# Rotary embedding on split heads: the cos and sin tables in 8 descriptors of 8 KB on partitions 0 to 31

## The chip, the cores and the metric

The kernel runs on one core of a Trainium2 chip. The core has a matrix engine (TensorE, PE in the profile), a vector engine (VectorE, DVE), a scalar engine (ScalarE, ACT), GpSimd (POOL) and SyncE (SP), which here only issues transfers. 16 DMA engines move data between the chip's memory (HBM) and the core's on-chip memory of 128 partitions. The metric is the device time of one execution in microseconds.

## The reference

```python
batch, seq, dim = 16, 512, 1024          # x: float32
num_heads = 16                           # head_dim 64, half_dim 32
# cos, sin: [seq, half_dim], float32
x = x.reshape(batch, seq, num_heads, head_dim)
x1, x2 = x[..., :half_dim], x[..., half_dim:]
cos = cos[None, :, None, :]
sin = sin[None, :, None, :]
rotated = np.concatenate([
    x1 * cos - x2 * sin,
    x1 * sin + x2 * cos
], axis=-1)
```

Every element of x is read once and every element of the output written once: 33.55 MB each way. cos and sin are 64 KB each; all batches and all heads share them, so a row of the tables belongs to a position in the sequence.

## The kernel before, in words

**Tiling.** The input is cut into 8 slabs of two batches each. A slab is 4.19 MB of float32: 128 partitions of 8192 numbers (32 KB), eight consecutive positions of the sequence (`rpp` = 8) per partition. Five float32 buffers hold slabs (`slots` = 5). Two bfloat16 buffers (`xpool`, tag "xb", 16 KB per partition) hold the slab that is being worked on.

**Loads and stores.** SP issues the loads of slabs 0 to 5 (line 64), POOL those of slabs 6 and 7. Loads 0 to 4 are issued at the start, load 0 first. Load s + 5 reuses the buffer of slab s and so waits until store s has landed. ACT issues the stores (line 151), and at the start, behind load 0, the two table loads (line 80).

**Tables.** Partition p needs the table rows of its own eight positions, and partitions 64 apart need the same ones. The kernel does not load them in that form. It loads each table as `TR` = 16 rows of 1024 float32 (4 KB): cos to partitions 0, 8, ..., 120 of the tile `raw`, sin to partitions 4, 12, ..., 124. `raw` has been set to zero before by DVE (line 72), and POOL casts it to bfloat16 (`raw_b`, line 102). Then TensorE spreads the rows: POOL has built one-hot matrices in `pick` (a memset, line 92, and 12 selects, line 96; three kinds g for cos, sin and minus sin, and `TQ` = 4 quarters j of a row), and for each of four parts of the accumulator `acc` four matmuls (line 107) pick for every partition the row and quarter that it needs: 16 matmuls of 128 by 128 by 256. DVE copies `acc` to the bfloat16 table `tab` (line 113). Every multiply reads `tab`.

**Work on a slab.** ACT casts it to bfloat16 (line 122). DVE multiplies twice by parts of `tab` (line 143; the product with the sine goes into the slab's own buffer) and adds with the halves exchanged (line 146). ACT casts the result back to float32 into the slab's buffer (line 149) and issues the store. Slabs 0, 6 and 7 are worked on in two halves, the others whole. ACT's order is written out by the loop: the cast of the next piece, then the write-back of the current one, then the store.

There is no planner. Each engine and each queue does its instructions in the order of the program, and each instruction waits for the data and buffers that it needs.

Of the kernel before, what the change touches and what calls it, by code (L numbers as in the profile page):

```python
# [2 lines left out]

# [4 lines left out]


@with_exitstack  # L10
def kernel(
    ctx: ExitStack,
    tc: tile.TileContext,
    x: bass.AP,
    cos: bass.AP,
    sin: bass.AP,
    num_heads: int,
    out: bass.AP,
):
    nc = tc.nc  # L20
    P = nc.NUM_PARTITIONS

    batch, seq, dim = x.shape
    nh = num_heads
    hd = dim // nh
    half = hd // 2
    bf16 = mybir.dt.bfloat16
    f32 = mybir.dt.float32

    nb = 2  # L30
    slots = 5
    nslabs = batch // nb
    rpp = nb * seq // P
    W = rpp * dim
    SP = seq // rpp
    TW = rpp * half

    out_flat = out.rearrange("b s h d -> b s (h d)")

    singles = ctx.enter_context(tc.tile_pool(name="singles", bufs=1))  # L40
    slabs = ctx.enter_context(tc.tile_pool(name="slabs", bufs=slots))
    xpool = ctx.enter_context(tc.tile_pool(name="xpool", bufs=2))
    psum = ctx.enter_context(tc.tile_pool(
        name="psum", bufs=1, space=bass.MemoryType.PSUM))


    def dram(t, s, a=0, n=W):
        return bass.AP(tensor=t.tensor, offset=t.offset + s * nb * seq * dim + a,
                       ap=[[W, P], [1, n]])


    def view(t, offset, *dims):
        return dataclasses.replace(t, offset=t.offset + offset,
                                   ap=[t.ap[0], *[list(d) for d in dims]])


    slab = {}


    def load(s):  # L60

        queue = nc.sync if s < nslabs - 2 else nc.gpsimd
        slab[s] = slabs.tile([P, W], f32, tag="slab", name="slab")
        queue.dma_start(out=slab[s], in_=dram(x, s))  # L64

    TR = 16
    TQ = seq // TR // rpp
    TC = seq * half // TR  # L70
    raw = singles.tile([P, TC], f32, tag="raw")
    nc.vector.memset(raw, 0.0)  # L72


    def load_tables(queue):
        for i, src in enumerate((cos, sin)):
            to = dataclasses.replace(
                raw, offset=raw.offset + 4 * i * raw.ap[0][0],
                ap=[[P // TR * raw.ap[0][0], TR], [1, TC]])
            queue.dma_start(out=to, in_=bass.AP(  # L80
                tensor=src.tensor, offset=src.offset, ap=[[TC, TR], [1, TC]]))


    load(0)
    load_tables(nc.scalar)
    for s in range(1, slots):
        load(s)

    pick = singles.tile([P, 3 * TQ * P], bf16, tag="pick")
    nc.gpsimd.memset(pick, 0.0)  # L92
    for g in range(3):
        for j in range(TQ):
            part = view(pick, (g * TQ + j) * P + j, (SP, P // SP), (TQ, TR))
            nc.gpsimd.affine_select(  # L96
                out=part, in_=part, compare_op=mybir.AluOpType.not_equal,
                fill=-1.0 if g == 2 else 1.0, base=-4 if g else 0,
                pattern=[[0, P // SP], [-(P // TR), TR]], channel_multiplier=1)

    raw_b = singles.tile([P, TC], bf16, tag="raw_b")
    nc.gpsimd.tensor_copy(out=raw_b, in_=raw)  # L102

    acc = psum.tile([P, 2 * rpp * hd], f32, tag="acc")
    for g, at in ((0, 0), (0, half), (1, rpp * hd), (2, rpp * hd + half)):
        for j in range(TQ):
            nc.tensor.matmul(  # L107
                view(acc, at, (hd, rpp), (1, half)),
                view(pick, (g * TQ + j) * P, (1, P)),
                view(raw_b, j * TW, (half, rpp), (1, half)),  # L110
                start=j == 0, stop=j == TQ - 1)
    tab = singles.tile([P, 2 * rpp * hd], bf16, tag="tab")
    nc.vector.tensor_copy(out=tab, in_=acc)  # L113

    xb = {}


    def cast(u):
        s, r, n = u
        if r == 0:  # L120
            xb[s] = xpool.tile([P, W], bf16, tag="xb", name="xb")
        nc.scalar.copy(out=view(xb[s], r * dim, (1, n * dim)),  # L122
                       in_=view(slab[s], r * dim, (1, n * dim)))

    passes = []
    for s in range(nslabs):
        n = rpp if 1 <= s < nslabs - 2 else rpp // 2  # L130
        passes += [(s, r, n) for r in range(0, rpp, n)]


    cast(passes[0])
    for i, (s, r, n) in enumerate(passes):
        if i + 1 < len(passes):
            cast(passes[i + 1])
        xs = view(slab[s], r * dim, (1, n * dim))
        xu = view(xb[s], r * dim, (1, n * dim))

        t2 = view(slab[s].bitcast(bf16), 2 * r * dim, (1, n * dim))
        for t, a in ((t2, rpp * hd), (xu, 0)):
            nc.vector.tensor_mul(  # L143
                out=t, in0=xu,
                in1=view(tab, a + r * hd, (hd, n), (0, nh), (1, hd)))
        nc.vector.tensor_add(  # L146
            out=xu, in0=xu, in1=view(t2, half, (hd, n * nh), (-half, 2), (1, half)))

        nc.scalar.copy(out=xs, in_=xu)  # L149
        if r + n == rpp:  # L150
            nc.scalar.dma_start(out=dram(out_flat, s), in_=slab[s])  # L151
            if s + slots < nslabs:
                load(s + slots)


# [1 line left out]
_INS = ['x', 'cos', 'sin', 'num_heads']  # L157
_OUTS = [((16, 512, 16, 64), 'float32')]

_NUMBERS = {'num_heads': 16}  # L160


# [26 lines left out]
```

## Time and profile before

| | |
|---|---|
| median of 3 runs | 162.08 us (161.93 to 162.35) |
| span of the profiled execution, first to last instruction | 161.0 us |
| moved | 67.24 MB, mean 418 GB/s |
| busy: ACT, DVE, POOL, PE | 113.6, 109.3, 5.9, 3.6 us |
| sin table landed, after its issue | 10.3 us |
| first multiply starts | 19.02 us |
| stores issued (slab 0, 1, 2, 7) | 38.10, 52.90, 67.25, 146.00 us |

The profiled execution is listed by its span; what the median has above it, 1.1 us, lies outside the first and last instruction. The profile's time line is in microseconds from the start of the span. A row of it gives start, duration, engine, line, operation, output and inputs, and in brackets how long the engine had been idle and what ended that. A stretch of time gives the busy time of each engine in it, the clock that TensorE was granted, the busy share of the 16 DMA engines, and GB/s; a packet is counted where it starts, so a short stretch can show a share slightly over 1. The DMA rows give a queue (q1 for SP's transfers, q10 for ACT's, q0 for POOL's), its packets, MB, and the time of its packets as a share of 16 engines over the stretch. A slab's packet is a partition's 32 KB. Packets of a few bytes are the completions.

### The profile page before, as it was taken

To read this page: it belongs to the slowest core of one execution; us is meant where nothing else is said; L and a number is where in the kernel's file an instruction comes from. 1 tells how busy PE (TensorE), PEld (TensorE's weight loads), DVE (VectorE), ACT (ScalarE), POOL (GpSimd) and SP (SyncE) were. 2 spreads that over 40 slices of the span, in tenths; PEclk is the share of its full clock that TensorE was granted. 3 is DMA by queue.
4 is the path that set the end of the run, shared out by engine and by line. 5 is a ranking of instruction groups with operands and counts; after the bars stand their busy time and mean duration, and the time that the engine had idled before them with its cause. 6 is when DMAs were issued, how large, how long until landed. Compare 5 with 4: busy or idle time off the path is not lost.

```text
span 161.0 us, 204 instructions
## 1 busy us (share of the span) xinstructions
PE 3.6 (2%) x16; PEld 2.3 (1%) x16; DVE 109.3 (68%) x35; ACT 113.6 (71%) x23; POOL 5.9 (4%) x20
## 2 busy tenths in 40 slices
PE   0005300000000000000000000000000000000000
PEld 0003100000000000000000000000000000000000
DVE  2000599999999969997998089949739599930000
ACT  2104939998999899899926998089995999562000
POOL 8002000000000000000010001000000000000000
DMA  6999999999999999999999999999999999999993
GB/s 228 423 383 423 399 464 440 399 456 440 407 432 456 415 423 456 423 415 464 391 415 432 456 415 432 448 423 432 448 423 432 440 432 432 440 423 440 440 423 147
DMA packets 2368, 67.24 MB, mean 418 GB/s; under 512 B 288, under 2 KB 288, under 8 KB 320
## 3 DMA queue, kind: packets, MB, share of 16 engines
q10 hardware_dynamic: 1216, 33.69, 48.5%
q1 hardware_dynamic: 864, 25.17, 37.2%
q0 software_dynamic: 288, 8.39, 12.1%
HBM read 33.69 MB, written 33.55 MB: 418 GB/s over the span
## 4 chain that ended last, share of the span: by engine, by line
DMA 42%; DVE 21%; ACT 20%; issue 4%; PE 2%; POOL 1%; ACTq 1%; POOLq 0%; DVEq 0%
DMA out_dram<-slab 20%; DMA slab<-in_x_dram 15%; ACT slab L149 13%; DVE xb L143 7%; DVE slab L143 7%; ACT xb L122 7%; DMA raw<-in_sin_dram 6%; DVE xb L146 6%; PE acc L107 2%; DVE tab L113 1%; POOL raw_b L102 1%; DVE raw L72 1%; ACTq L80 0%; ACTq L151 0%; POOLq L102 0%
## 5 line engine op out<-in xcount | busy, mean ns | idle before, releaser
L122 ACT CAST xb<-slab 128x4096 bf16<-128x4096 f32 (+1 forms) x11 | 56.6, 5155 | 25.3 <-DMA slab<-in_x_dram 24.1
L149 ACT CAST slab<-xb 128x4096 f32<-128x4096 bf16 (+1 forms) x11 | 56.6, 5154 | 3.8 <-DVE xb L146 3.8
L143 DVE TENSOR_TENSOR slab<-xb,tab 128x4096 bf16<-128x4096 bf16 (+1 forms) x11 | 35.9, 3260 | 15.5 <-ACT xb L122 15.3
L146 DVE TENSOR_TENSOR xb<-xb,slab 128x4096 bf16<-128x4096 bf16 (+1 forms) x11 | 35.9, 3260 | 0.3
L143 DVE TENSOR_TENSOR xb<-xb,tab 128x4096 bf16<-128x4096 bf16 (+1 forms) x11 | 35.9, 3260 | 0.3
L113 DVE CAST tab<-acc 128x1024 bf16<-128x1024 f32 x1 | 1.2, 1225 | 15.8 <-PE acc L107 15.8
L64 POOL DMA_DIRECT2D slab<-in_x_dram x2 | 1.2, 611 | 85.4 <-DMA out_dram<-slab 66.8
L107 PE MATMUL acc<-raw_b,pick 128*128 128x256 bf16 x16 | 3.6, 418 | 14.1 <-POOL raw_b L102 14.1
L122 ACT ACT_TABLE_LOAD x1 | 1.3, 1283 | 3.2 <-issue 3.2
L107 PEld LDWEIGHTS <-pick 128*128 128x128 bf16 x16 | 2.3, 145 | 14.9 <-issue 11.5
L96 POOL TENSOR_SCALAR_AFFINE_SELECT pick<-pick 128x32 bf16<-128x32 bf16 x12 | 2.1, 248 | 0.1
L72 DVE MEMSET raw<- 128x1024 f32 x1 | 0.9, 912 | 1.0 <-PEq L170 1.0
L92 POOL MEMSET pick<- 128x1536 bf16 x1 | 1.4, 1379 | 0.3 <-POOLq L170 0.3
L102 POOL CAST raw_b<-raw 128x1024 bf16<-128x1024 f32 x1 | 1.0, 1037 | 8.7 <-DMA raw<-in_sin_dram 8.7
L170 POOL MEMSET const-float32-0.0<- 128x1 f32 x1 | 0.1, 99 | 0.2 <-issue 0.2
L170 POOL MEMSET const-bfloat16-1.0<- 128x1 bf16 x1 | 0.1, 102 | 0.0
L170 POOL MEMSET const-uint8-127<- 128x1 uint8 x1 | 0.1, 102 | 0.0
L170 POOL MEMSET const-float32-1.0<- 128x1 f32 x1 | 0.1, 99 | 0.0
## 6 DMA issues: line engine op xcount, KB each, us to landing
out_dram<-slab ACTq DMA_DIRECT2D x8, 4096.0 KB, 26.1
slab<-in_x_dram SPq DMA_DIRECT2D x6, 4096.0 KB, 28.2
slab<-in_x_dram POOLq DMA_DIRECT2D x2, 4096.0 KB, 24.5
raw<-in_cos_dram ACTq DMA_DIRECT2D x1, 64.0 KB, 8.1
raw<-in_sin_dram ACTq DMA_DIRECT2D x1, 64.0 KB, 10.3
```

The source lines that it names most:

```text
L64: queue.dma_start(out=slab[s], in_=dram(x, s))
L72: nc.vector.memset(raw, 0.0)
L92: nc.gpsimd.memset(pick, 0.0)
L96: nc.gpsimd.affine_select(out=part, in_=part, compare_op=mybir.AluOpType.not_equal, fill=-1.0 if g == 2 else 1.0, base=-4 if g else 0, pat ...
L102: nc.gpsimd.tensor_copy(out=raw_b, in_=raw)
L107: nc.tensor.matmul(view(acc, at, (hd, rpp), (1, half)), view(pick, (g * TQ + j) * P, (1, P)), view(raw_b, j * TW, (half, rpp), (1, half)), ...
L113: nc.vector.tensor_copy(out=tab, in_=acc)
L122: nc.scalar.copy(out=view(xb[s], r * dim, (1, n * dim)), in_=view(slab[s], r * dim, (1, n * dim)))
L143: nc.vector.tensor_mul(out=t, in0=xu, in1=view(tab, a + r * hd, (hd, n), (0, nh), (1, hd)))
L146: nc.vector.tensor_add(out=xu, in0=xu, in1=view(t2, half, (hd, n * nh), (-half, 2), (1, half)))
L149: nc.scalar.copy(out=xs, in_=xu)
L170: nc = _bacc.Bacc("TRN2", target_bir_lowering=False, num_devices=1)
```

## The change

Each table is loaded as 8 rows of 2048 float32 (8 KB) instead of 16 rows of 4 KB: cos to partitions 0, 4, ..., 28 and sin to 1, 5, ..., 29. The rows, in float32 and as bfloat16, no longer have tiles of their own. They lie in one of the two "xb" buffers, which is not in use at that time and becomes the buffer of slab 1 afterwards. DVE's memset and POOL's cast now work on 32 partitions and 2048 columns, where they had 128 partitions and 1024 columns. A row now holds eight groups of positions (`TQ` = 8), so there are 24 selects of 16 elements instead of 12 of 32, `pick` is twice as long (3072 columns), and 32 matmuls, with 32 rows each, take the place of 16 with 128 rows.

```diff
-    TR = 16
+    TR = 8
+    TS = 4
+    TK = TR * TS
     TQ = seq // TR // rpp
     TC = seq * half // TR
-    raw = singles.tile([P, TC], f32, tag="raw")
-    nc.vector.memset(raw, 0.0)
+    tmp = xpool.tile([P, W], bf16, tag="xb", name="tmp")
+    raw = view(tmp.bitcast(f32), 0, (1, TC))
+    raw_b = view(tmp, 2 * TC, (1, TC))
+    nc.vector.memset(raw[0:TK], 0.0)
...
             to = dataclasses.replace(
-                raw, offset=raw.offset + 4 * i * raw.ap[0][0],
-                ap=[[P // TR * raw.ap[0][0], TR], [1, TC]])
+                raw, offset=raw.offset + i * raw.ap[0][0],
+                ap=[[TS * raw.ap[0][0], TR], [1, TC]])
...
-                fill=-1.0 if g == 2 else 1.0, base=-4 if g else 0,
-                pattern=[[0, P // SP], [-(P // TR), TR]], channel_multiplier=1)
+                fill=-1.0 if g == 2 else 1.0, base=-1 if g else 0,
+                pattern=[[0, P // SP], [-TS, TR]], channel_multiplier=1)
...
-    raw_b = singles.tile([P, TC], bf16, tag="raw_b")
-    nc.gpsimd.tensor_copy(out=raw_b, in_=raw)
+    nc.gpsimd.tensor_copy(out=raw_b[0:TK], in_=raw[0:TK])
...
             nc.tensor.matmul(
                 view(acc, at, (hd, rpp), (1, half)),
-                view(pick, (g * TQ + j) * P, (1, P)),
-                view(raw_b, j * TW, (half, rpp), (1, half)),
+                view(pick, (g * TQ + j) * P, (1, P))[0:TK],
+                view(raw_b, j * TW, (half, rpp), (1, half))[0:TK],
                 start=j == 0, stop=j == TQ - 1)
```

## The prediction

> **What bounds the kernel now.** Read the page first: its span, the three rows of busy engines, the row of DMA and the bytes. Then the stretches of time, to see whether the transfers ever pause.
>
> ```profile
> span 161.0 us, 204 instructions
> DVE  2000599999999969997998089949739599930000
> ACT  2104939998999899899926998089995999562000
> DMA  6999999999999999999999999999999999999993
> HBM read 33.69 MB, written 33.55 MB: 418 GB/s over the span
> ```
>
> ```profile
> 0.00:1.80 1.80, 0.00 (x0) 0.00 (x0) 0.78 (x1) 0.00 (x0) 1.27 (x5) 1.00 0.21 55
> 6.00:12.00 6.00, 0.00 (x0) 0.00 (x0) 0.00 (x0) 0.00 (x0) 0.00 (x0) 1.00 1.07 421
> 20.00:40.00 20.00, 0.00 (x0) 0.00 (x0) 19.90 (x8) 16.98 (x5) 0.00 (x0) 1.00 1.02 437
> 100.00:124.00 24.00, 0.00 (x0) 0.00 (x0) 17.76 (x7) 17.54 (x4) 0.53 (x1) 1.00 1.00 433
> 149.00:157.00 8.00, 0.00 (x0) 0.00 (x0) 0.00 (x0) 0.00 (x0) 0.00 (x0) 1.00 1.01 438
> ```
>
> The last two columns are the DMA share and GB/s. Once the first slab is on its way, all 16 DMA engines work without a pause at 420 to 438 GB/s until about 158 us. 67.24 MB at 433 GB/s is 155.3 us, so the span of 161.0 is that, 1.8 us before the first byte, and about 4 us of slow start, uneven finish and last landing. The transfers bound the kernel. DVE and ACT rest for tens of microseconds each. The span lies 1.1 us under the median of the runs, 162.08; I add that 1.1 to every sum.
>
> The change works in the first 24 us, in what leads to the first multiply:
>
> ```profile
> 1.02 0.91 DVE L72 MEMSET raw<- 128x1024 f32 x1 [1.02 <-PEq L170]
> 1.96 0.56 ACTq L80 DMA_DIRECT2D raw<-in_cos_dram  x1
> 2.56 0.61 ACTq L80 DMA_DIRECT2D raw<-in_sin_dram  x1
> 12.99 1.04 POOL L102 CAST raw_b<-raw 128x1024 bf16<-128x1024 f32 x1 [8.72 <-DMA raw<-in_sin_dram]
> 14.08 3.57 PE L107 MATMUL acc<-raw_b,pick 128*128 128x256 bf16 x16 [14.08 <-POOL raw_b L102]
> 17.69 1.23 DVE L113 CAST tab<-acc 128x1024 bf16<-128x1024 f32 x1 [15.76 <-PE acc L107]
> ```
>
> Each waits for the one above; the first multiply starts at 19.02 us. While they wait, the DMA engines are loading slabs 0 to 4, for which nothing here is needed.
>
> **The change, part by part, on the path to the first multiply.**
> - Memset: 1024 f32 columns took 0.91 us; 2048 on 32 partitions take 0.91 (if partitions counted) to 1.82. I take 1.82: +0.91 on the issue of both tables.
> - Landing: cos landed 8.1 us after its issue, sin 10.3, though 64 KB need 0.15 us at 433 GB/s. They wait in turn behind 32 KB slab packets of 1.2 us each. The later issue adds 0.91, or a whole turn of 1.2, or nothing if the packet still catches its turn; and only 8 of the descriptors' owners must answer instead of 16, so the slowest may drop out, a turn less. I take 0, with -1.2 and +1.2 as ends.
> - Cast on POOL: 1.04 us for 1024 columns, so 2.07 for 2048: +1.04 (0 if partitions counted).
> - Picking tables: the memset of 1536 columns took 1.38 us, 3072 take 2.76; 24 selects at the 0.17 us spacing of the present 12 take 4.2. POOL is done at 7.7 instead of 4.3 us, under its 8.7 us wait for sin: 0.
> - Matmuls: 16 take 3.57 us, one every 0.21. Their moving side stays 256 columns, so 32 take 6.93: +3.36 (0 if 32 rows were four times as fast).
> - The copy to tab has the same shape: 0.
>
> Sum: first multiply at 19.02 + 1.04 + 3.36 = 23.4 us, 4.4 later (ends -1.2 and +5.8). The Trainium skill (TensorE: Matmul & The Clock Gate, Part 1: The HAM clock gate (the "warmup" mystery)) has TensorE at half clock for some 3.4 us of steady work and at full clock after. By it the second 16 matmuls would take about 1.7 us, an estimate, and the sum would be 2.7 instead of 4.4. The page's clock column stands at 1.00 and the 16 matmuls here show no step, but their burst is only 3.57 us long, so no run here shows it.
>
> The shared buffer adds one wait: ACT's cast of slab 1 (24.04 us, when the slab lands) now waits for the last matmul. That ends near 17.67 + 4.4 = 22.1, 1.9 us earlier. Behind that cast stand ACT's two write-backs of slab 0, which wait for DVE anyway: 0; if matmuls end after 24.0, the cover is gone.
>
> **What the 4.4 us do further on.** DVE's pass over slab 0 ends at 37.0 instead of 32.6, so ACT's second write-back (3.6 us) ends at 40.6 and store 0 is issued 2.5 us later than 38.1, since ACT had to wait for nothing there before but its own cast. Stores 1, 2 and 3 come the full 4.4 later (57.3, 71.7, 86.0). None of this empties the DMA queues: five slabs are 20.97 MB, 48.4 us at 433 GB/s, so loads alone last until about 51 us, and store 0 could be 10 us late. Store 0 landed at 61.5 (issue 38.1 and 23.4), load 4 at about 64 (longest time to landing, 61.3, from its issue near 2.8). Together they carry the same bytes in either order, so store 0 lands no later than 64: load 5 is issued 0 to 2.5 us later, and I take 1.3. Loads 5, 6 and 7 follow one another at half rate (cast at 85.95, 105.32, 124.68), so slab 7 arrives about 1.3 later too, and from there it is a bare chain to the last store: 146.00 becomes 147.3.
>
> ```profile
> 124.68 3.60 ACT L122 CAST xb<-slab 128x4096 bf16<-128x4096 f32 x1 [1.82 <-DMA slab<-in_x_dram]
> 142.37 3.60 ACT L149 CAST slab<-xb 128x4096 f32<-128x4096 bf16 x1 [3.47 <-DVE xb L146]
> 146.00 0.34 ACTq L151 DMA_DIRECT2D out_dram<-slab  x1
> out_dram<-slab ACTq DMA_DIRECT2D x1, 4096.0 KB, 14.1
> ```
>
> Does that show at the end? The last store landed 14.1 us after its issue. Its own 4.19 MB need 9.7 us, the first load shows 1.0 us from issue (0.74) to first byte (about 1.75), and I put 0.5 on its final receipt: so it queued 2.9 us behind store 6. With engines that finish over about 1.2 us (the DMA share is 0.99 from 157 to 158 us and 0.31 in the next), 1.7 us of lateness cost nothing. 1.3 is inside: 0 us.
>
> **What the tables take from the DMA engines.** This is on the path. Beside them the slab packets slow down:
>
> ```profile
> q1 hardware_dynamic: 73, 2.39, 101.0%
> q10 hardware_dynamic: 62, 0.13, 5.9%
> ...
> q1 hardware_dynamic: 299, 8.75, 101.6%
> ```
>
> The first two rows are 6 to 12 us, the last 20 to 40 (32 of its 299 packets are completions). 73 packets in 101% of 96 engine-us are 1.33 us each, against 1.22 later: 0.11 x 73 / 16 = 0.5 us lost per engine. The tables' own packets take 5.9% of 6 us, 0.35 us per engine. An 8 KB descriptor is twice a 4 KB one, and eight of them leave some engines without. An engine with one of each table gives 0.7 us instead of 0.35, one without gives 0; on both, the 0.5 may stay (same bytes), vanish (fewer packets) or double (twice the size). So the engine with tables changes by -0.15 to +0.85, the one without by -0.85 to +0.15. The last engine sets the end; no view here names it. With the 0.5 unchanged it is +0.35 or -0.35, and I take 0 between.
>
> Sum: 161.0 + 0 + 0 = 161.0 in the span, 162.1 us as the runs count. The forecast is no change: within 0.3% (0.5 us), which is about what a measurement of this kernel can tell from none.
>
> **Rivals.**
> - **Tables cost the DMA engines less.** Fewer and larger packets disturb the slabs less, and the last engine is one without tables. For it: the slow packets lie exactly where the tables do. Against: the bytes are the same. The most is 0.85; I price it at 0.6: 161.5 us.
> - **Tables crowd eight engines.** If an engine's loss grows with the table bytes that it carries itself, 0.85 becomes 1.7 on eight engines, and one of these ends last: 162.9 us. Against it: the 0.5 now falls on packets ahead of an engine's own table too. The Trainium skill (DMA: Bandwidth & Descriptors, Rules for kernel authors) speaks against the change here: a copy whose outermost dimension is under 16 runs on no more engines than that. No run of before has such a copy; by it each of the eight carries 16 KB and the rest none, as assumed in this rival.
> - **The last store is late.** If the 4.4 us pass whole to slab 7, the last store is issued at 150.4, and 4.4 less the 1.7 to 2.9 of slack is 1.5 to 2.7: about 164.1 us. It decides from 147.7 us on. For it: the chain of waits does run from the tables through ACT to the last store. Against: that chain passes twice through transfers that share a full pipe, and the bound on store 0 cuts it to 2.5.
> - **The split is undone.** If the 8 rows were cut into 16 pieces again, the DMA side is as before and the 4.4 us hidden: 162.1, part of the forecast.
>
> **How the numbers follow.** Forecast 0.47 (0.42 within 0.3%, 0.03 below, 0.02 above), cheaper tables 0.24, crowding 0.14, late store 0.15. So faster 0.27, same 0.42, slower 0.31. The forecast's own range is 161.6 to 162.6. The range of 161.2 to 163.4 takes in the full 0.85 gained, crowding, and the mild end of the late store, and leaves out about 0.14 above and 0.05 below.
>
> **What the changed profile would show.** Memset 1.8 us, POOL cast 2.1, 32 matmuls 5 to 7 us, first multiply 22 to 24.5, store 0 near 40.6: right about the start. Last store at 146 to 147.7 and DMA at 430 GB/s or more throughout: right about the cover. Wrong if DMA falls below that between 40 and 150 us, if the last store lands within 11.5 us of its issue (nothing ahead of it), or if the slab packets between 6 and 13 us take far more or less than 1.33 us.

## The result, and the profile after

The changed kernel takes 163.34 us (median of 22 runs, 162.58 to 164.12); the kernel before, run in turn with it, 162.36 us (22 runs, 161.93 to 163.31). The ratio is 1.0048, with an interval of 1.0035 to 1.0062: **slower by 0.5%, 0.8 us**. The two medians are 1.0 us apart; the text goes by the ratio. The forecast was no change, within 0.3%, at 162.1 us. The measured change is larger than that and clear of the noise; the time lies just inside the stated range of 161.2 to 163.4 us.

The profiled execution has a span of 162.1 us and took 163.86 us, so 1.8 us lie around the span. From its page:

```profile
span 162.1 us, 263 instructions
DMA  7999999989999999998999999999999999999990
q14 instruction: 1, 0.01, 0.0%
HBM read 33.69 MB, written 33.55 MB: 415 GB/s over the span
DMA packets 2337, 67.25 MB, mean 415 GB/s; under 512 B 272, under 2 KB 272, under 8 KB 272
```

The DMA row has no gap: transfers still bound the kernel. One row is new: a single packet on a queue of kind "instruction", of which the page of before has none. In the trace it is 8 KB and starts at 162.06 us, as the span ends. The row of packets of before, for comparison:

```profile
DMA packets 2368, 67.24 MB, mean 418 GB/s; under 512 B 288, under 2 KB 288, under 8 KB 320
```

The time line of the changed kernel (start, duration, engine, line, operation, in brackets the wait before it):

```profile
1.22 1.76 DVE L76 MEMSET tmp<- 32x2048 f32 x1 [1.22 <-PEq L173]
3.02 1.22 ACTq L84 DMA_DIRECT2D tmp<-in_cos_dram  x1
3.47 3.87 POOL L100 TENSOR_SCALAR_AFFINE_SELECT pick<-pick 128x16 bf16<-128x16 bf16 x24
...
13.32 1.88 POOL L105 CAST tmp<-tmp 32x2048 bf16<-32x2048 f32 x1 [5.98 <-DMA tmp<-in_sin_dram]
...
15.25 6.98 PE L110 MATMUL acc<-tmp,pick 32*128 32x256 bf16 x32 [15.25 <-POOL tmp L105]
...
22.27 1.23 DVE L116 CAST tab<-acc 128x1024 bf16<-128x1024 f32 x1 [19.28 <-PE acc L110]
...
23.59 2.29 DVE L146 TENSOR_TENSOR slab<-xb,tab 128x4096 bf16<-128x4096 bf16 x1
...
40.86 0.35 ACTq L154 DMA_DIRECT2D out_dram<-slab  x1
...
62.45 0.33 SPq L64 DMA_DIRECT2D slab<-in_x_dram  x1
...
146.34 0.34 ACTq L154 DMA_DIRECT2D out_dram<-slab  x1
```

The first multiply starts at 23.59 us, 4.57 later than before; store 0 is issued at 40.86, 2.8 later; load 5 at 62.45, 0.9 later. The last store is issued only 0.34 us later than before. The last row of the issues gives how long it then took to land:

```profile
out_dram<-slab ACTq DMA_DIRECT2D x1, 4096.0 KB, 14.3
```

Before, that was 14.1 us. Stretches of time in the changed kernel (the last two columns are the DMA share and GB/s):

```profile
20.00:40.00 20.00, 2.23 (x11) 1.18 (x9) 17.57 (x8) 13.92 (x4) 0.00 (x0) 1.00 0.99 429
40.00:60.00 20.00, 0.00 (x0) 0.00 (x0) 19.81 (x6) 16.96 (x4) 0.00 (x0) 1.00 1.01 419
...
100.00:124.00 24.00, 0.00 (x0) 0.00 (x0) 20.09 (x8) 21.11 (x5) 0.53 (x1) 1.00 1.00 433
124.00:146.00 22.00, 0.00 (x0) 0.00 (x0) 18.16 (x8) 18.40 (x6) 0.00 (x0) 1.00 1.00 433
...
157.00:158.00 1.00, 0.00 (x0) 0.00 (x0) 0.00 (x0) 0.00 (x0) 0.00 (x0) 1.00 1.06 459
...
159.00:160.00 1.00, 0.00 (x0) 0.00 (x0) 0.00 (x0) 0.00 (x0) 0.00 (x0) 1.00 0.15 66
```

No stretch pauses, and 100 to 124 us moves 433 GB/s as before. From 40 to 60 us it moves less than before, at about the same share:

```profile
40.00:60.00 20.00, 0.00 (x0) 0.00 (x0) 18.97 (x5) 19.25 (x3) 0.00 (x0) 1.00 0.99 428
```

The end differs too: 66 GB/s for a microsecond is two packets of 32 KB, started while most engines are done. In the profiled execution of before that microsecond is empty, but so it is in the second profile of the changed kernel (`a0_after` below).

What becomes of the last 2 us is read from the instructions of the program's last source line, its closing (durations in ns as min/median/max, then first and last start in us). Before:

```profile
L184 POOLq DRAIN  x3: 34/93/24737, 100.0 to 160.7; - x3
L184 SPq DRAIN  x3: 7/7/7, 160.2 to 160.5; - x3
L184 POOLq EVENT_SEMAPHORE_RANGE_CLEAR  x1: 139/139/139, 160.5 to 160.5; - x1
```

And in the changed kernel:

```profile
L187 POOLq DRAIN  x3: 40/230/24290, 100.7 to 161.8; - x3
L187 SPq DRAIN  x3: 7/7/7, 160.8 to 161.1; - x3
L187 POOLq EVENT_SEMAPHORE_RANGE_CLEAR  x1: 139/139/139, 161.6 to 161.6; - x1
```

SP begins to drain when the last store has landed: at 160.2 before, at 160.8 now. POOL clears the semaphores 0.3 us later before, 0.8 us later now. So the 1.1 us between these two spans are 0.6 of a later landing and **0.5 of a longer closing**, in which no data move. In the trace the step is plain: when the last engine has been released from the barrier that follows SP's DRAIN, POOL's own DRAIN ends 0.12 us later in before and 0.62 us later now. Of these 0.5 us, 0.14 are the DRAIN itself (230 ns in place of 93); 0.36 pass before it starts, and nothing in the trace names what POOL does in them. The 0.6 of later landing is one execution against another; the 0.5 is what the experiments below test.

### The profile page after: what moved, and what is told of

Same layout as the page of the kernel before. It is cut to its first block, busy times and chain, and to the rows that moved or that the text cites. A ratio compares the mean times of both kernels' runs of the same rounds, so it can differ in the third digit from the quotient of the medians.

```text
span 162.1 us, 263 instructions
## 1 busy us (share of the span) xinstructions
PE 7.0 (4%) x32; PEld 4.5 (3%) x32; DVE 110.1 (68%) x35; ACT 113.8 (70%) x23; POOL 9.8 (6%) x32
## 4 chain that ended last, share of the span: by engine, by line
DMA 36%; DVE 23%; ACT 22%; PE 4%; issue 3%; POOL 1%; ACTq 1%; POOLq 0%; DVEq 0%; SPq 0%
DMA slab<-in_x_dram 17%; DMA out_dram<-slab 13%; ACT slab L152 13%; ACT xb L125 9%; DVE slab L146 7%; DVE xb L146 7%; DVE xb L149 7%; DMA tmp<-in_sin_dram 5%; PE acc L110 4%; POOL tmp L105 1%; DVE tmp L76 1%; DVE tab L116 1%; ACTq L84 1%; ACTq L152 0%; POOLq L105 0%
## 5 line engine op out<-in xcount | busy, mean ns | idle before, releaser
L110 PE MATMUL acc<-tmp,pick 32*128 32x256 bf16 x32 | 7.0, 412 | 15.2 <-POOL tmp L105 15.2
L110 PEld LDWEIGHTS <-pick 32*128 32x128 bf16 x32 | 4.5, 139 | 17.3 <-issue 15.2
L100 POOL TENSOR_SCALAR_AFFINE_SELECT pick<-pick 128x16 bf16<-128x16 bf16 x24 | 3.9, 255 | 0.1
L96 POOL MEMSET pick<- 128x3072 bf16 x1 | 2.7, 2658 | 0.3 <-POOLq L173 0.3
L76 DVE MEMSET tmp<- 32x2048 f32 x1 | 1.8, 1765 | 1.2 <-PEq L173 1.2
L105 POOL CAST tmp<-tmp 32x2048 bf16<-32x2048 f32 x1 | 1.9, 1879 | 6.0 <-DMA tmp<-in_sin_dram 6.0
```

The source lines that it names most:

```text
L76: nc.vector.memset(raw[0:TK], 0.0)
L100: nc.gpsimd.affine_select(out=part, in_=part, compare_op=mybir.AluOpType.not_equal, fill=-1.0 if g == 2 else 1.0, base=-1 if g else 0, pat ...
L105: nc.gpsimd.tensor_copy(out=raw_b[0:TK], in_=raw[0:TK])
L110: nc.tensor.matmul(view(acc, at, (hd, rpp), (1, half)), view(pick, (g * TQ + j) * P, (1, P))[0:TK], view(raw_b, j * TW, (half, rpp), (1, h ...
```

## The experiments

Each kernel was timed over five rounds against the kernel before on the same chip; the ratio and its interval are against that. The expectations were written as theories stood at the time, and they name them. The suspects were the transfers of the tables, the work that the change adds on DVE, POOL and TensorE, the later start of the slabs, and something outside the span.

**The kernel before against itself.** No edit.

> The kernel before, unchanged, to learn what lies around its span. Three theories of the 0.5% that the change cost. Outside: its 59 more instructions cost time before the first or behind the last one; then the time around the span is about 1.1 to 1.4 us here, against 1.77 us with the change. Crowding: eight DMA engines carry the tables and one of them ends last; then the time around the span is 1.77 us here too and the span is some 0.8 us shorter, near 160.7. Late start: the tables are ready 4.6 us later and a wait further on shows it; around the span 1.77 us as well, span near 160.7. All: ratio 1.000.

162.86 us against 162.15, ratio 1.0025 [1.0002, 1.0049], with 1.78 us around the span where the changed kernel has 1.77. Two things follow. Nothing of the 0.8 us lies outside the span. And two sets of runs of one kernel can differ by 0.25%: a ratio below that says nothing, and the interval is somewhat too narrow.

**The transfers of the change alone.** Tables in 8 rows of 8 KB into the idle buffer; memset, cast, selects and matmuls as before.

```diff
+    D8 = 8
+    DC = seq * half // D8
+    tmp = xpool.tile([P, W], bf16, tag="xb", name="tmp")
+    rows = view(tmp.bitcast(f32), 0, (1, DC))
+    raw = view(tmp.bitcast(f32), 0, (1, TC))
...
-                raw, offset=raw.offset + 4 * i * raw.ap[0][0],
-                ap=[[P // TR * raw.ap[0][0], TR], [1, TC]])
+                rows, offset=rows.offset + i * rows.ap[0][0],
+                ap=[[4 * rows.ap[0][0], D8], [1, DC]])
```

> Only the transfer of the change: 8 rows of 8 KB per table, to partitions 0, 4, ..., 28 and 1, 5, ..., 29 of the idle buffer. Memset, cast, selects and the 16 matmuls have the sizes of before, so the tables come out wrong. Outside: 1.000. Late start: 1.000 (landing moves by less than 0.5 us). Crowding: the whole 1.005, all in the span, and the last DMA packets end about 1 us after the others.

162.48 us, ratio 1.0018 [0.9994, 1.0041]: not to be told from before. The DMA queues from 6 to 12 us (packets, MB, share of 16 engines), in this kernel:

```profile
q1 hardware_dynamic: 80, 2.62, 101.1%
q10 hardware_dynamic: 32, 0.13, 5.3%
```

and in the changed kernel:

```profile
q1 hardware_dynamic: 78, 2.56, 98.6%
q10 hardware_dynamic: 31, 0.13, 5.3%
```

80 packets in 101.1% of 96 engine-us are 1.213 us each, and 78 in 98.6% are 1.214: the slabs' packets no longer slow down beside the tables, where before they took 1.33. The disturbance, 0.5 us per engine in the prediction, is gone, and the time is not shorter. The traces show where the gain goes. Between 40 and 50 us the 32 KB packets take 1.30 to 1.34 us in all five kernels' profiles with 8-row tables, and 1.21 to 1.23 in all nine with 16 rows. Eight packets per engine that are 0.08 to 0.12 us longer than before's 1.22 make 0.6 to 1.0 us, as much as was gained from 6 to 12 us or more. Why the packets lengthen there is not shown. So fewer, larger rows do from 6 to 12 us what the rival "Tables cost the DMA engines less" said, but buy nothing that can be measured.

**The computing of the change alone.** The changed kernel with 16 transfers of 4 KB.

```diff
-                raw, offset=raw.offset + i * raw.ap[0][0],
-                ap=[[TS * raw.ap[0][0], TR], [1, TC]])
+                raw, offset=raw.offset + 4 * i * raw.ap[0][0],
+                ap=[[8 * raw.ap[0][0], 16], [1, TC // 2]])
```

> The other half: both tables loaded as before (16 rows of 4 KB, spread over 128 partitions, into the idle buffer), with the memset, cast, 24 selects and 32 matmuls of the change; the tables come out wrong. Outside: 1.003 to 1.005 with 1.77 us around the span. Late start: 1.005, in the span, first multiply near 23.5 us. Crowding: 1.000.

163.23 us (7 runs), ratio 1.0056 [1.0035, 1.0076]: as much as the whole loss, though in the same comparison before itself stood at 1.0025. So it points at the computing, not at the transfers. In its trace the closing is late too: POOL's DRAIN ends 0.62 us behind the barrier.

**More work on TensorE.** The kernel before with 16 further matmuls behind its own.

```diff
+    more = psum.tile([P, rpp * half], f32, tag="more")
+    for j in range(16):
+        nc.tensor.matmul(
+            view(more, 0, (1, rpp * half)), view(pick, 0, (1, P)),
+            view(raw_b, 0, (1, rpp * half)), start=j == 0, stop=j == 15)
```

> The kernel before with 16 more matmuls behind its own, into a bank that nobody reads: 32 more instructions on TensorE, off every path. Outside: the time around the span rises by half or more of the difference, ratio 1.002 to 1.004. Crowding and late start: 1.000.

162.52 us, ratio 1.0013 [0.9993, 1.0033], closing 0.12 us: more instructions on TensorE are not it.

**The changed kernel again**, as the partner of the runs that follow.

> The changed kernel again, beside the three that follow. Theory Tail: POOL's 12 additional selects make its instruction stream longer, and after the last store has landed POOL's closing DRAIN ends some 0.6 us behind the barrier in place of 0.1; that is 0.5 us of the change's cost. Theory Late: the tables are ready 4.6 us later and this reaches the end. Theory Crowding: eight DMA engines carry the tables and one of them ends last. All three: ratio 1.004 to 1.006, with the closing DRAIN late.

163.49 us against 162.68, ratio 1.0038 [1.0017, 1.0058]. Closing 0.63 us.

**More instructions on POOL.** The kernel before with 12 small memsets on POOL behind the selects.

```diff
+    spare = singles.tile([P, 32], bf16, tag="spare")
+    for k in range(12):
+        nc.gpsimd.memset(spare, 0.0)
```

> The kernel before with 12 small memsets more on POOL, on a tile that nobody reads, beside idle time. Tail: POOL's closing DRAIN ends 0.5 us later behind the barrier, as with the change, ratio 1.003. Late and Crowding: closing as before, ratio 1.000.

162.65 us, ratio 1.0016 [0.9993, 1.0039]. The closing keeps its 0.12 us. But 2.06 us lie around the span in place of 1.80: 0.26 us in another place. The pages count 32 busy instructions of POOL in this kernel and in the changed one, but that is not all of its instructions. In the trace a MOVE on POOL's sequencer goes with every select, so 12 more selects are 24 more instructions and 12 memsets are 12: before has 204 in all, this kernel 216, and before with 24 selects (below) 228. So this run rules out 12 more instructions as the cause, and not the number that the change adds.

**The changed kernel with 3 selects in place of 24.** One select for each kind g, over all eight groups at once; nothing else differs.

```diff
-        for j in range(TQ):
-            part = view(pick, (g * TQ + j) * P + j, (SP, P // SP), (TQ, TR))
-            nc.gpsimd.affine_select(
-                out=part, in_=part, compare_op=mybir.AluOpType.not_equal,
-                fill=-1.0 if g == 2 else 1.0, base=-1 if g else 0,
-                pattern=[[0, P // SP], [-TS, TR]], channel_multiplier=1)
+        part = view(pick, g * TQ * P, (P + 1, TQ), (SP, P // SP), (TQ, TR))
+        nc.gpsimd.affine_select(
+            out=part, in_=part, compare_op=mybir.AluOpType.not_equal,
+            fill=-1.0 if g == 2 else 1.0, base=-1 if g else 0,
+            pattern=[[0, TQ], [0, P // SP], [-TS, TR]], channel_multiplier=1)
```

> The changed kernel with the same pick matrices made by 3 selects of 128 elements in place of 24 of 16; transfers, cast and 32 matmuls as with the change. Tail: the closing is as before the change, ratio 1.001 to 1.003, and at least 0.5 us under the changed kernel beside it. Late and Crowding: no gain, 1.004 to 1.006.

162.75 us, ratio 1.0009 [0.9983, 1.0034], and 0.74 us under the changed kernel beside it. Its closing:

```profile
L186 POOLq DRAIN  x3: 34/93/24987, 99.8 to 160.4; - x3
L186 SPq DRAIN  x3: 7/7/7, 159.9 to 160.2; - x3
L186 POOLq EVENT_SEMAPHORE_RANGE_CLEAR  x1: 139/139/139, 160.3 to 160.3; - x1
```

From SP's first DRAIN to the clearing it is 0.4 us, and DRAIN's median is back at 93 ns. The memset of 32 partitions, the long cast, 32 matmuls, the first multiply 4.6 us late and the tables in 8 rows are all still there, and cost nothing that can be measured.

**The same, repeated.**

> The changed kernel with 3 selects once more, for what is left of the change without its 24 selects: transfers in 8 descriptors and a start 4.6 us later. Tail alone: 1.000 to 1.001. Crowding or Late as a second cause: 1.002 to 1.003.

162.62 us, ratio 1.0003 [0.9979, 1.0027]; its closing is short as well.

**The kernel before with 24 selects.** Each of its 12 selects is cut in two halves of 16 elements; tables, matmuls and the late start stay out.

```diff
-            part = view(pick, (g * TQ + j) * P + j, (SP, P // SP), (TQ, TR))
-            nc.gpsimd.affine_select(
-                out=part, in_=part, compare_op=mybir.AluOpType.not_equal,
+            for h in range(P // SP):
+                half_part = view(pick, (g * TQ + j) * P + j + h * SP, (TQ, TR))
+                nc.gpsimd.affine_select(
+                    out=half_part, in_=half_part,
+                    compare_op=mybir.AluOpType.not_equal,
...
-                pattern=[[0, P // SP], [-(P // TR), TR]], channel_multiplier=1)
+                    pattern=[[-(P // TR), TR]], channel_multiplier=1)
```

> The kernel before, with each of its 12 selects cut into two of 16 elements: the same matrices, 24 selects, and nothing else touched. Tail: POOL's range clear at the very end comes 0.5 us or more behind SP's last DRAIN, where it came within 0.1 before; ratio 1.003. If only the number of POOL's instructions counted, and not where its stream ends, the 12 memsets would have shown this too; they did not, so Tail stands or falls here. Otherwise 1.000.

162.99 us, ratio 1.0024 [1.0004, 1.0044]. Its closing, and a row of its page:

```profile
L186 POOLq DRAIN  x3: 40/237/24417, 99.7 to 160.9; - x3
L186 SPq DRAIN  x3: 7/7/7, 159.9 to 160.2; - x3
L186 POOLq EVENT_SEMAPHORE_RANGE_CLEAR  x1: 139/139/139, 160.7 to 160.7; - x1
```

```profile
q14 instruction: 1, 0.01, 0.0%
```

0.8 us from the first DRAIN to the clearing, DRAIN's median at 237 ns, POOL's DRAIN 0.62 us behind the barrier, and the instruction packet: the selects alone bring back the closing of the changed kernel. The ratio by itself would not carry this, since a kernel against itself gave 1.0025; the place in the trace does, and the ratio agrees with it (0.5 us are 0.3%). The expectation takes the 12 memsets as proof that the number of instructions does not count. They are no proof, for they add half as many. Counted with the sequencer's, POOL has 31 instructions with 3 selects, 49 with 12, 61 with 12 and the memsets, and 73 with 24; only the last have the late closing. That POOL's program must pass some length is as good an account as that it must hold many selects.

**The kernel before with 3 selects.** The same edit as in the changed kernel, with the strides of 16 rows.

> The kernel before with its pick matrices made by 3 selects of 128 elements in place of 12 of 32. Tail: the closing is already at its short form, so 1.000; if POOL's stream cost anything more, up to 0.3 us faster, 0.998.

162.59 us, ratio 0.9993 [0.9969, 1.0016]. 12 selects and 3 have the same closing, so there is nothing to gain here: it is a step that comes between 12 and 24 selects, not a price per select.

**The slabs' start made late in the kernel before.** 22 matmuls ahead of its own, and in a second kernel 66.

```diff
+    more = psum.tile([P, rpp * half], f32, tag="more")
+    for j in range(22):
+        nc.tensor.matmul(
+            view(more, 0, (1, rpp * half)), view(pick, 0, (1, P)),
+            view(raw_b, 0, (1, rpp * half)), start=j == 0, stop=j == 21)
```

> The kernel before with 22 matmuls ahead of its own (22 x 0.21 = 4.6 us), so that the first multiply starts near 23.6 us; the transfers and POOL are those of before. Late: ratio 1.004 to 1.006, in the span. Tail and Crowding: 1.000, the last store issued within 1.5 us of 146 and the DMA engines without a pause.

162.86 us (10 runs; 163.59 with the two longest of the twelve), ratio 1.0027 [0.9989, 1.0064]: unclear. The first multiply came at 22.25 us, 3.2 late and not the 4.6 aimed at, for the matmuls became faster on the way. The spans of its twelve runs fall in two groups of six, 160.3 to 161.2 and 162.5 to 164.9, and the profiled one is of the upper.

> The kernel before with 66 matmuls ahead of its own, so that the first multiply starts 8 to 10 us later. The cover worked out in the prediction (store 0 may come 10 us late, the last store 1.7 us): at most 1.003, DMA without a pause until 140 us. Late: the cost grows with the delay, 1.01 or more.

163.66 us, ratio 1.0053 [1.0022, 1.0084], with the first multiply at 25.56 us, 6.5 late. Its spans fall in two groups of six as well, 160.7 to 161.4 and 162.3 to 162.8; here the profiled one is of the lower. None of the 35 runs of before beside it is over 161.6. In the profile the last store is issued at 145.79, earlier than in before, and the closing takes 0.12 us. From 60 to 80 us, with 22 matmuls and then with 66:

```profile
60.00:80.00 20.00, 0.00 (x0) 0.00 (x0) 17.67 (x5) 19.59 (x4) 0.00 (x0) 0.50 1.00 400
```

```profile
60.00:80.00 20.00, 0.00 (x0) 0.00 (x0) 18.62 (x5) 19.59 (x3) 0.69 (x1) 0.50 1.00 421
```

The DMA share is 1.00 in both, but they move 400 and 421 GB/s; in that stretch before moved 426 and the changed kernel 431. In the profile of the upper group the engines never pause, their packets last longer, around the time when load 5 joins the stores: 26 GB/s less than before over 20 us are 0.5 MB, or 1.2 us. The profile of the lower group shows little of it. So with a late start about half of the executions take some 1.5 us longer, and the medians say little; what decides between the groups, these runs do not settle. For the changed kernel it is no explanation: with 3 selects its start is 4.6 us late, none of those 24 runs has a span over 161.9, and the cost is gone.

## Where the prediction held and where it failed

That 163.34 us lies inside the stated range, by 0.06 us, is luck: the upper end was there for crowding and for a late last store, and neither came. The forecast itself, no change within 0.5 us, did not hold. Of the 1.2 us between it and the measured time, 0.3 are the kernel before, whose median over 22 runs is 162.36 and not 162.08.

**The step that failed is "Picking tables ... 0".** It let 12 more selects vanish under POOL's wait for the sine table, and that part is right: the selects end near 7.3 us and POOL waits 5.98 us afterwards. What it did not see is that the longer program of POOL shows again 150 us later, after the last byte: its DRAIN in the closing ends 0.5 us later. Removing the selects removes both the late closing and the loss (1.0009 and 1.0003); adding them alone to the kernel before brings the late closing back. That is shown. Why the DRAIN ends later is not. A packet of kind "instruction" at the end of the span goes with it in every trace: it is on the pages of the changed kernel, twice, and of the 24 selects alone; with the change's computing alone the trace has it at 161.56 us, just behind the last instruction, where the page no longer counts it; and none of the ten traces with 12 or 3 selects has it. That suggests instructions being fetched, but its start lies behind the DRAIN, not before it, so it is not shown to be what POOL waited for.

**The start** came as worked out: memset 1.76 us (1.82), cast 1.88 (2.07), matmuls 6.98 (6.93), first multiply 23.59 (23.4), store 0 at 40.86 (40.6). The cast began 0.33 us later, where the landing's 0 had it at no change. The alternative sum of 2.7 us by the clock gate did not come: 32 matmuls in 6.98 us are 0.218 us each, with no step.

**The cover held.** Load 5 came 0.9 us later (1.3), the last store 0.34 (1.3), 14.3 us to its landing, DMA without a pause. One sign that was to speak against it did come: from 40 to 60 us DMA fell to 419 GB/s, below the 430 that the prediction asked for. The changed kernel with 3 selects shows 419 there as well, without a loss of time, so the sign does not mark the cost. "The last store is late" did not happen: it was to decide from 147.7 us on, and the issue was at 146.34. The kernel with 22 added matmuls does say that the step judged the cover by pauses alone, and that packets can lengthen without one.

**What the tables take** was mis-sized: the disturbance of 0.5 us per engine vanished (1.21 us a packet in place of 1.33), where the sum left it unchanged and took 0. "Tables cost the DMA engines less" had that part right and the time wrong: longer packets between 40 and 50 us take the gain back. "Tables crowd eight engines" finds no support: the transfers alone gave 1.0018, and with 3 selects the same transfers gave 1.0009 and 1.0003. That its 162.9 us lies nearer to the result than the forecast is chance. Its premise holds in part: 32 packets fewer on the page, 16 data and 16 completions, beside one instruction packet more, so each table has 8 completions in place of 16. The Trainium skill (DMA: Bandwidth & Descriptors, Rules for kernel authors) has a copy with eight outer rows run on at most eight engines, and these rows agree with it; whether both tables use the same eight, the traces do not tell. That such an engine would end last by 0.85 us no run shows: in one profile of the changed kernel two packets end 1 us behind the others, in the other none do.

**Around the span** the term of 1.1 us was mis-sized: it is 1.8 us in every kernel but the one with 12 memsets (2.06). The profiled execution of before, span 161.0, was simply a slow one against its median. The sum's own comparison was hardly hurt, since both kernels carry the same 1.8.

In all: of 0.8 us, 0.5 is the closing, shown; the remaining 0.3 is of the size by which a kernel differs from itself.

## What to carry to other kernels

An instruction that is hidden where it runs may still be paid for where the program ends: when a change multiplies the instructions of an engine, look at the closing of the program, after the last transfer, in both traces, and count the sequencer's instructions too. Ask for one instruction with a longer pattern before splitting work into many small ones; 3 selects did here what 24 did. And run the unchanged kernel against itself before giving a cause to a difference of a quarter per cent.

## What the runs showed of the hardware that was not expected

- 24 selects on POOL lengthen the closing from 0.12 to 0.62 us behind the barrier; 3 and 12 leave it at 0.12, and so do 12 selects with 12 small memsets, which add 0.26 us around the span. Every select has a MOVE of the sequencer with it.
- Matmuls with 128 rows speed up in the middle of a burst, those with 32 rows did not. With 66 added matmuls, the time line of TensorE has

```profile
13.73 8.73 PE L106 MATMUL more<-raw_b,pick 128*128 128x256 bf16 x66 [13.73 <-POOL raw_b L102]
22.29 1.91 PE L112 MATMUL acc<-raw_b,pick 128*128 128x256 bf16 x16
```

  that is 0.13 us each over the first burst and 0.12 in the second, against 0.22 in before's 3.57 us. The Trainium skill (TensorE: Matmul & The Clock Gate, Part 1: The HAM clock gate (the "warmup" mystery)) has the change come around 4 us into steady work, give or take half a microsecond. Here it came 2.8 us after the first matmul of this burst, 5.8 us with 22 added matmuls and 5.4 us with the 16 behind before's own, so it is seen, but over a wider range. The 32 matmuls of 32 rows stayed at 0.218 us through 6.98 us. The five sets of runs with them, 65 runs, all have a mean granted clock of 1.00, where 51 of 100 runs of before have about 0.56. No run separates the number of rows from the rest of that kernel.
- The column of the granted clock reads 1.00 through such a burst, for slow and fast matmuls alike, and 0.50 from 2 to 3 us after its end.
- In before, table rows of 4 KB spread over 128 partitions made the slabs' packets beside them 1.33 us long; rows of 8 KB to partitions 0 to 31 left them at 1.21, and the packets between 40 and 50 us became longer instead (1.30 to 1.34 us, against 1.21 to 1.23). Which of size, number and place does it was not separated.
